# Which PSUM banks the convolution's norm uses, and where the first chunk's pieces land

## The chip, the cores and the metric

The kernel runs on one core of one Trainium2 chip. The metric is the device time of one execution in microseconds (us), as the median of several runs. A profiled execution gives the trace of that core.

## The reference

The reference is one layer of a conformer-like block on 256 tokens of width 1024, all in float32:

```
x = x + 0.5 * swiglu(rms_norm(x), w_gate, w_up, w_down)            # FFN 1, inner width 2816
proj = rms_norm(x) @ w_in                                           # 1024 -> 7168
a, b, q, k, v, gate_a, gate_b = split(proj)
u = causal_depthwise_conv(a * sigmoid(b))                           # 31 taps, 1024 channels
y_a = silu(layer_norm(u) * gain + bias) @ w_conv_proj
y_b = attention(rms_norm(q), rms_norm(k), v) @ w_attn_proj          # 16 heads of 64, causal
x = x + (sigmoid(gate_a) * y_a + sigmoid(gate_b) * y_b) @ w_out
x = x + 0.5 * swiglu(rms_norm(x), w_gate2, w_up2, w_down2)          # FFN 2
```

With 256 tokens and blocks of 256 the attention has one block, so only its causal own part is computed.

## The kernel before, in words

**Products.** Every product is made with operands split in two: `hi` is the value rounded to a short float32 form, `lo` is the rest. A product is the sum of three: activation hi x weight hi, activation hi x weight lo, activation lo x weight hi. The function `gemm` (L137) loads a piece of weights, two slices of 128 input rows by 512 columns, from memory into a "raw" buffer (SP issues the load, L151), rounds it to `hi` on ScalarE (ACT, L100), subtracts to make `lo` on VectorE (DVE) or GpSimd (POOL) (L102), and runs for each of two token halves and each slice three 128x512 matmuls on TensorE (PE, L165 to L167). The buffers "raw", "hi" and "lo" are rings of five. A chunk is 512 output columns: its products over all input rows end in two accumulators, one for each token half.

**PSUM.** The eight banks have three uses, each a ring: three banks "acc" for `gemm`, three "tr" for transposes and attention, two "cv" for the convolution and, at the very start, for the first chunk.

**The start.** The first chunk of FFN 1 has a function of its own, `gemm_first` (L106). Its eight pieces hold 512 columns of weights for one slice and, except the first, that slice of the transposed input (256 columns). Each goes through a "raw" buffer; ACT scales and rounds the input (L125), DVE makes its rest (L126), ACT rounds the weights and DVE makes their rest (L100, L102), PE runs six products into the two "cv" banks (L132 to L134). The second chunk goes through `gemm`; the loads of x and of the constants are queued on SP behind the second chunk's last piece (L597).

**The mixing block.** The projection `w_in` has 14 chunks. Between their products the kernel interleaves the attention of eight head pairs (score L465, flip L512, value L529, whose result ACT copies at L220), all in "tr" banks, and the convolution (L347, on DVE, one tap at a time for two channel slices into two "cv" banks, which ACT copies out at L350). A generator per channel group goes on a list, and `gemm` pumps a few steps of it after each piece. Behind the last convolution `conv_norm` (L352) stands on that list: for each token half two groups of four transposes into a "tr" bank (L359), a copy to SBUF by ACT (L364), statistics on DVE (L368, L370), the power -1/2 on POOL (L187) and the normalization on DVE (L375).

**The end of the mixing block.** Two chunks of the attention's projection (`w_attn`) follow; behind the last attention block ACT applies the sigmoid to gate b (L703), and DVE multiplies each accumulator by it (L714). Ahead of the second chunk the program places `conv_act` (L378): four times four transposes back into a "tr" bank (L385), SiLU on ACT (L392), rounding on ACT (L398) and the rest on DVE (L399). Its SiLUs are ordered behind the sigmoids of gate b, and the sigmoids of gate a behind what it returns, since each change between the two functions makes ACT load a table. Then come the convolution's projection (`w_conv`, two chunks, DVE L722 and L723) and `w_out`.

**What sets the order.** The program is written once in order; a planner then simulates the engines and fixes the order of each engine's queue. An instruction earlier in the program goes first among those that the planner takes to be ready, and a tile takes a buffer of its ring when its first writer is placed. On the chip each queue is executed in that fixed order.

Of the kernel before, what the change touches and what calls it, by code (L numbers as in the profile page):

```python
# [11 lines left out]
F32 = mybir.dt.float32  # L12
# [5 lines left out]
P = 128  # L18
S = 256
D = 1024  # L20
KD = D // P
# [7 lines left out]
CH = 512  # L29
# [6 lines left out]
KP = 2  # L36
RAW_BUFS, HI_BUFS, LO_BUFS = 5, 5, 5
# [13 lines left out]
class Build:  # L51
# [54 lines left out]
    def gemm_first(self, x0, w0, rest, hT):  # L106

        nc = self.nc
        acc = [self.cv(), self.cv()]
        hTh, hTl = hT  # L110
        ah, al = self.parts(*hT)
        for k in range(KD):
            raw = self.wp.tile([P, KP * CH], F32, tag="raw", name="raw", bufs=RAW_BUFS)
            hi = self.wp.tile([P, KP * CH], F32R, tag="hi", name="hi", bufs=HI_BUFS)
            lo = self.wp.tile([P, KP * CH], F32R, tag="lo", name="lo", bufs=LO_BUFS)
            if k == 0:
                nc.sync.dma_start(x0, self.io["x0"])
                nc.sync.dma_start(raw[:, :CH], w0)
                xk = x0[:, KD:]
            else:  # L120
                self.last_dma = nc.sync.dma_start(raw[:, : CH + S], rest[:, k - 1, :])
                xk = raw[:, CH : CH + S]
            g = x0[:, k : k + 1]
            sl = slice(k * S, (k + 1) * S)
            nc.scalar.activation(hTh[:, sl], xk, AF.Copy, scale=g)  # L125
            nc.vector.scalar_tensor_tensor(  # L126
                hTl[:, sl], xk, g, hTh[:, sl].bitcast(F32), ALU.mult, ALU.subtract
            )
            self.split(raw[:, :CH], hi[:, :CH], lo[:, :CH], False)
            for t in range(2):  # L130
                o, st, sp = acc[t], k == 0, k == KD - 1
                nc.tensor.matmul(o, ah(k, t), hi[:, :CH], start=st, stop=False)  # L132
                nc.tensor.matmul(o, ah(k, t), lo[:, :CH], start=False, stop=False)
                nc.tensor.matmul(o, al(k, t), hi[:, :CH], start=False, stop=sp)  # L134
        return acc

    def gemm(self, w, c, n, kt, ah, al, pump=0, pool=0.0, split_k=None, side=None):  # L137
# [214 lines left out]
    def conv_norm(self, yT, ynat):  # L352
        nc = self.nc
        for t in range(2):
            for c0 in range(0, KD, 4):
                ps = self.tr()
                for q in range(4):
                    c = c0 + q
                    nc.tensor.transpose(  # L359
                        ps[:, q * P : (q + 1) * P],  # L360
                        yT[c // 2][:, (c % 2) * S + t * P : (c % 2) * S + (t + 1) * P],
                        self.ident,
                    )
                nc.scalar.copy(ynat[:, t * D + c0 * P : t * D + (c0 + 4) * P], ps)  # L364
                yield 1
            st = self.tmp.tile([P, 2, 6], F32, tag="bst", name="bst", bufs=2)
            for c in range(2):
                nc.vector.bn_stats(st[:, c, :], ynat[:, t * D + c * CH : t * D + (c + 1) * CH])  # L368
            mv = self.tmp.tile([P, 2], F32, tag="mv", name="mv", bufs=2)
            nc.vector.bn_aggr(mv, st)  # L370
            r = self.rsqrt_mean(mv[:, 1:2], 1, 1)
            yield 1
            for c in range(2):
                y = ynat[:, t * D + c * CH : t * D + (c + 1) * CH]
                nc.vector.tensor_scalar(y, y, mv[:, 0:1], r, ALU.subtract, ALU.mult)  # L375
            yield 1

    def conv_act(self, ynat, hi, lo, after):  # L378
        nc = self.nc
        cst = self.cst  # L380
        for c in range(0, KD, 2):
            ps = self.tr()
            for q in range(2):
                for t in range(2):
                    nc.tensor.transpose(  # L385
                        ps[:, q * S + t * P : q * S + (t + 1) * P],
                        ynat[:, t * D + (c + q) * P : t * D + (c + q + 1) * P], self.ident,
                    )
            z = self.tmp.tile([P, CH], F32, tag="junk", name="z", bufs=2)
            with self.tc.issue_after(after.ins):  # L390
                for q in range(2):
                    last = nc.scalar.activation(  # L392
                        z[:, q * S : (q + 1) * S], ps[:, q * S : (q + 1) * S], AF.Silu,
                        bias=cst[:, C_LB + c + q : C_LB + c + q + 1],
                        scale=cst[:, C_LG + c + q : C_LG + c + q + 1],
                    )
            h = hi[:, c * S : (c + 2) * S]
            nc.scalar.copy(h, z)  # L398
            nc.vector.tensor_tensor(lo[:, c * S : (c + 2) * S], z, h.bitcast(F32), ALU.subtract)  # L399
        return last  # L400


    def head_norm(self, acc, rstd, c, dst, gain, rq=None):
# [437 lines left out]
```

## Time and profile before

| what | us |
|---|---|
| median of 3 runs | 647.08 |
| lowest and highest | 646.92, 647.13 |
| profiled execution | 647.48 |
| its span in the trace | 645.6 |

Times in the trace are counted from the start of the span. The profiled execution has its own time, 647.48; the span is what the instructions take, and the rest lies around it. A line of the timeline gives start, duration, engine, line of the kernel and operation, the tile written and those read, how many instructions were merged, and in brackets the idle time of the engine before it and what ended it. A matmul's duration includes the filling and emptying of the array, so starts, not durations, tell the pace of PE.

### The profile page before, as it was taken

What the parts mean: (1) busy time and instruction counts of PE and PEld (TensorE: products, weight loads), DVE (VectorE), ACT (ScalarE), POOL (GpSimd) and SP (SyncE); (2) the same over time, 40 slices, a digit from 0 to 9 for tenths busy, and PEclk for the clock granted to TensorE, in tenths of its full rate; (3) what the DMA queues carried; (4) which work ended last, traced back from release to release, by engine and by line L of the source; (5) the groups of instructions that cost most, each with busy time, mean ns of one, the idle gap of its engine ahead of it and who ended that gap; (6) DMA issues with size and microseconds to landing.
All of it is one profiled execution on the core that took longest, in us unless ns stands there. A gap on an engine that the chain in (4) does not pass through costs nothing.

```text
span 645.6 us, 8133 instructions
## 1 busy us (share of the span) xinstructions
PE 634.2 (98%) x2952; PEld 516.8 (80%) x2952; DVE 369.9 (57%) x625; ACT 362.5 (56%) x547; POOL 164.9 (26%) x83
## 2 busy tenths in 40 slices
PE   9999999999999999999999997899999999999997
PEld 7788888888888888777777785788888888888886
DVE  5655464554542699879313936485664546465541
ACT  6755354443545676987876667744655435444330
POOL 0100000000006999689866761000100000000000
PEclk9999999999999999999999999799999999999999
DMA  8966556567564555545654552264755656556630
GB/s 271 354 232 192 199 173 195 160 198 219 174 201 135 178 170 180 171 130 169 196 158 135 164 168 96 96 199 153 224 163 186 196 177 198 189 168 200 197 124 32
DMA packets 32855, 114.97 MB, mean 178 GB/s; under 512 B 3632, under 2 KB 4912, under 8 KB 32816
## 3 DMA queue, kind: packets, MB, share of 16 engines
q1 hardware_dynamic: 32816, 114.46, 55.9%
q8 instruction: 23, 0.38, 0.2%
q14 instruction: 16, 0.13, 0.1%
HBM read 113.40 MB, written 1.05 MB: 177 GB/s over the span
## 4 chain that ended last, share of the span: by engine, by line
PE 64%; DVE 2%; ACT 1%; issue 0%; DVEq 0%
PE acc L165 20%; PE acc L166 20%; PE acc L167 19%; PE tr L465 1%; PE tr L211 1%; PE tr L529 1%; PE tr L512 1%; DVE lo L102 1%; PE tr L438 1%; DVE bst L368 0%; ACT gate_b L703 0%; ACT z L392 0%; PE tr L655 0%; DVE gate_b L714 0%; ACT L703 0%
## 5 line engine op out<-in xcount | busy, mean ns | idle before, releaser
L100 ACT CAST hi<-raw 128x1024 fp32r<-128x1024 f32 (+1 forms) x216 | 223.1, 1035 | 220.3 <-PE acc L167 184.4
L102 DVE TENSOR_TENSOR lo<-raw,hi 128x1024 fp32r<-128x1024 f32 (+1 forms) x156 | 186.2, 1197 | 167.2 <-ACT hi L100 162.7
L102 POOL TENSOR_TENSOR lo<-raw,hi 128x1024 fp32r<-128x1024 f32 x60 | 143.7, 2420 | 200.3 <-ACT hi L100 200.2
L347 DVE SCALAR_TENSOR_TENSOR cv<-uT,cst,cv 128x255 f32<-128x255 f32 (+28 forms) x240 | 95.2, 465 | 8.4 <-ACT cv L343 8.2
L166 PE MATMUL acc<-lo,h1h 128*128 128x512 f32 x224 | 88.3, 394 | 0.0
L165 PE MATMUL acc<-hi,h1h 128*128 128x512 f32 x224 | 88.0, 398 | 0.2 <-DVE un L646 0.2
L167 PE MATMUL acc<-hi,h1l 128*128 128x512 f32 x224 | 87.3, 393 | 0.0
L165 PE MATMUL acc<-hi,h2h 128*128 128x512 f32 x176 | 69.1, 393 | 0.0
L165 PE MATMUL acc<-hi,aTh 128*128 128x512 f32 x176 | 68.8, 391 | 0.0
L167 PE MATMUL acc<-hi,aTl 128*128 128x512 f32 x176 | 68.5, 389 | 0.0
L166 PE MATMUL acc<-lo,aTh 128*128 128x512 f32 x176 | 68.5, 389 | 0.0
L166 PE MATMUL acc<-lo,h2h 128*128 128x512 f32 x176 | 68.5, 390 | 0.0
L167 PE MATMUL acc<-hi,h2l 128*128 128x512 f32 x176 | 67.2, 390 | 0.0
L166 PE MATMUL acc<-lo,hTh 128*128 128x512 f32 x160 | 62.4, 390 | 0.5 <-DVE lo L102 0.5
L165 PE MATMUL acc<-hi,hTh 128*128 128x512 f32 x160 | 62.2, 392 | 0.0
L167 PE MATMUL acc<-hi,hTl 128*128 128x512 f32 x160 | 62.2, 389 | 0.0
L165 PEld LDWEIGHTS acc<-hi,h1h 128*128 128x128 f32 x224 | 42.1, 188 | 10.3 <-issue 0.7
L167 PEld LDWEIGHTS acc<-hi,h1l 128*128 128x128 f32 x224 | 42.1, 188 | 9.3 <-issue 0.7
L166 PEld LDWEIGHTS acc<-lo,h1h 128*128 128x128 f32 x224 | 42.1, 188 | 8.9 <-issue 0.8
L167 PEld LDWEIGHTS acc<-hi,aTl 128*128 128x128 f32 x176 | 33.0, 188 | 6.9
L165 PEld LDWEIGHTS acc<-hi,aTh 128*128 128x128 f32 x176 | 33.0, 188 | 6.8
L165 PEld LDWEIGHTS acc<-hi,h2h 128*128 128x128 f32 x176 | 33.0, 188 | 6.8
(138 smaller groups left out, 778.8 us busy)
## 6 DMA issues: line engine op xcount, KB each, us to landing
raw<-w_in SPq DMA_DIRECT2D x56, 512.0 KB, 4.2
raw<-w2gu SPq DMA_DIRECT2D x44, 512.0 KB, 4.4
raw<-w1gu SPq DMA_DIRECT2D x40, 512.0 KB, 4.8
raw<-w1d SPq DMA_DIRECT2D x22, 512.0 KB, 4.3
raw<-w2d SPq DMA_DIRECT2D x22, 512.0 KB, 4.4
raw<-w_attn SPq DMA_DIRECT2D x8, 512.0 KB, 4.2
raw<-w_conv SPq DMA_DIRECT2D x8, 512.0 KB, 4.0
raw<-w_out SPq DMA_DIRECT2D x8, 512.0 KB, 4.4
```

Source lines behind the costliest of these rows:

```text
L100: nc.scalar.copy(hi, raw)
L102: ins = eng.tensor_tensor(lo, raw, hi.bitcast(F32), ALU.subtract)
L165: nc.tensor.matmul(o, ah(k, t), wh, start=st, stop=False)
L166: nc.tensor.matmul(o, ah(k, t), wl, start=False, stop=False)
L167: nc.tensor.matmul(o, al(k, t), wh, start=False, stop=sp)
L211: nc.tensor.transpose(ps[:, q * S + t * P : q * S + (t + 1) * P], src(t, j + q), self.ident)
L347: nc.vector.scalar_tensor_tensor(o, u, w, o, ALU.mult, ALU.add)
L438: nc.tensor.transpose(ps[:, q * S + t * P : q * S + (t + 1) * P], xs[t][:, (j + q) * P : (j + q + 1) * P], self.ident,)
L465: ins = nc.tensor.matmul(ps[q][:, t * P : t * P + (t + 1) * P], qT[r, b * S + t * P : b * S + (t + 1) * P], kT[r, b * S : b * S + (t + 1) ...
L512: nc.tensor.transpose(ps[:, i * P : (i + 1) * P], pr[:, o : o + P], self.ident)
L529: ins = nc.tensor.matmul(ps[q * HD : (q + 1) * HD, kt * P : S], v[:, kt * D + h * HD : kt * D + (h + 1) * HD], pT[:, o : o + n], start=kt ...
```

## The change

Three edits. The first chunk's pieces land in four tiles of 128x2048 of the pool that also holds the activations (two pieces in each), in place of "raw" buffers. Its products come in another order: for both token halves those with `hi` weights, then those with `lo` weights. The transposes of `conv_norm` and `conv_act` go to "cv" banks in place of "tr" banks, and `conv_act` returns its last rounding in place of its last SiLU, so that the sigmoids of gate a are ordered behind that.

```diff
@@ gemm_first
-            raw = self.wp.tile([P, KP * CH], F32, tag="raw", name="raw", bufs=RAW_BUFS)
+            if k % 2 == 0:
+                pair = self.big("first")
+            raw = pair[:, (k % 2) * 1024 : (k % 2) * 1024 + CH + S]
...
             for t in range(2):
-                o, st, sp = acc[t], k == 0, k == KD - 1
-                nc.tensor.matmul(o, ah(k, t), hi[:, :CH], start=st, stop=False)
-                nc.tensor.matmul(o, ah(k, t), lo[:, :CH], start=False, stop=False)
-                nc.tensor.matmul(o, al(k, t), hi[:, :CH], start=False, stop=sp)
+                nc.tensor.matmul(acc[t], ah(k, t), hi[:, :CH], start=k == 0, stop=False)
+                nc.tensor.matmul(acc[t], al(k, t), hi[:, :CH], start=False, stop=False)
+            for t in range(2):
+                nc.tensor.matmul(acc[t], ah(k, t), lo[:, :CH], start=False, stop=k == KD - 1)
@@ conv_norm
-                ps = self.tr()
+                ps = self.cv()
@@ conv_act
-            ps = self.tr()
+            ps = self.cv()
...
-                    last = nc.scalar.activation(
+                    nc.scalar.activation(
                         z[:, q * S : (q + 1) * S], ps[:, q * S : (q + 1) * S], AF.Silu,
...
             h = hi[:, c * S : (c + 2) * S]
-            nc.scalar.copy(h, z)
+            rounded = nc.scalar.copy(h, z)
             nc.vector.tensor_tensor(lo[:, c * S : (c + 2) * S], z, h.bitcast(F32), ALU.subtract)
-        return last
+        return rounded
```

## Rows read from the trace of the kernel before

**Rows 1.** The page, busy us, share of the span and instructions of PE.
```profile
PE 634.2 (98%) x2952; PEld 516.8 (80%) x2952; DVE 369.9 (57%) x625; ACT 362.5 (56%) x547; POOL 164.9 (26%) x83
```
**Rows 2.** Timeline of PE, first and second chunk.
```profile
10.96 0.61 PE L132 MATMUL cv<-hi,hTh 128*128 128x512 f32 x2
...
16.40 0.67 PE L165 MATMUL acc<-hi,hTh 128*128 128x512 f32 x2
17.60 0.50 PE L166 MATMUL acc<-lo,hTh 128*128 128x512 f32 x1 [0.53 <-DVE lo L102]
```
**Rows 3.** Timeline of ACT, first and second chunk.
```profile
8.55 0.60 ACT L100 CAST hi<-raw 128x512 fp32r<-128x512 f32 x1
...
15.24 1.05 ACT L100 CAST hi<-raw 128x1024 fp32r<-128x1024 f32 x1 [2.24 <-PE cv L134]
```
**Rows 4.** Timeline of SP's queue, second chunk's loads.
```profile
9.91 3.32 SPq L151 DMA_DIRECT2D raw<-w1gu  x4
```
**Rows 5.** Windows: busy PE, PEld, DVE, ACT, POOL; granted clock, DMA share, GB/s.
```profile
5.00:10.00 5.00, 5.00 (x21) 3.18 (x19) 3.90 (x8) 3.90 (x8) 0.00 (x0) 1.00 0.96 352
10.00:15.00 5.00, 5.00 (x23) 4.17 (x23) 3.88 (x8) 3.00 (x7) 0.00 (x0) 1.00 0.92 266
```
**Rows 6.** Windows of the end of the mixing block, columns as above.
```profile
381.60:388.70 7.10, 7.10 (x44) 5.09 (x43) 0.42 (x1) 1.31 (x4) 3.84 (x2) 1.00 0.62 205
...
392.00:394.00 2.00, 1.34 (x7) 0.61 (x6) 0.91 (x2) 2.00 (x6) 0.00 (x0) 1.00 0.00 0
...
404.00:406.00 2.00, 0.82 (x4) 0.82 (x5) 1.59 (x3) 0.00 (x0) 0.00 (x0) 0.50 0.95 336
...
410.00:412.00 2.00, 2.00 (x9) 1.58 (x8) 0.00 (x0) 1.98 (x4) 0.00 (x0) 0.86 0.02 4
```
**Rows 7.** Timeline of PE, end of the mixing block.
```profile
388.59 1.09 PE L359 MATMUL tr<-ident,uT 128*128 128x128 f32 x8
...
391.73 0.95 PE L167 MATMUL acc<-hi,ol 128*128 128x512 f32 x3
393.11 0.66 PE L359 MATMUL tr<-ident,uT 128*128 128x128 f32 x4 [0.43 <-ACT ynat L364]
394.43 0.50 PE L165 MATMUL acc<-hi,oh 128*128 128x512 f32 x1 [0.66 <-DVE gate_b L714]
...
401.50 0.76 PE L385 MATMUL tr<-ident,ynat 128*128 128x128 f32 x3 [1.33 <-ACT ms L185]
405.18 3.13 PE L385 MATMUL tr<-ident,ynat 128*128 128x128 f32 x13 [2.93 <-DVE ynat L375]
408.62 0.80 PE L165 MATMUL acc<-hi,u2h 128*128 128x512 f32 x1 [0.30 <-ACT u2h L398]
...
410.49 0.44 PE L165 MATMUL acc<-hi,u2h 128*128 128x512 f32 x1
```
**Rows 8.** Timeline of ACT, end of the mixing block.
```profile
377.55 0.37 ACT L350 COPY uT<-cv 128x256 f32<-128x256 f32 x1
...
388.71 0.37 ACT L220 CAST oh<-tr 128x256 fp32r<-128x256 f32 x1 [4.41 <-PE tr L529]
...
390.39 2.19 ACT L703 ACTIVATE gate_b<-gate_b 128x512 f32<-128x512 f32 x4
392.49 1.54 ACT L364 COPY ynat<-tr 128x512 f32<-128x512 f32 x3
...
406.12 1.93 ACT L392 ACTIVATE z<-tr,cst 128x256 f32<-128x256 f32 x4 [3.43 <-PE tr L385]
407.94 1.15 ACT L398 CAST u2h<-z 128x512 fp32r<-128x512 f32 x2
```
**Rows 9.** Timelines of DVE and POOL, the norm.
```profile
393.09 0.69 DVE L368 BATCH_NORM_STATS2 bst<-ynat 128x6 f32<-128x512 f32 x1 [3.55 <-ACT ynat L364]
...
404.59 1.00 DVE L375 TENSOR_SCALAR ynat<-ynat,mv,rs 128x512 f32<-128x512 f32 x2
...
401.48 1.88 POOL L187 TENSOR_TENSOR rs<-ms,neghalf 128x1 f32<-128x1 f32 x1 [1.38 <-ACT ms L185]
```

## The prediction

> **What bounds the kernel now.** I read the page first, for the share of each engine: TensorE (PE) is busy for 98% of the span [rows 1], so time can only come from stretches in which it waits or runs slowly. Then the busy time by windows, to find those stretches, the timeline of PE around them, and the timelines of the engines that PE waits for.
>
> The pace of PE is read from the first chunk: the step k = 4 starts at 10.96 and the next chunk at 16.40 [rows 2]; 24 products lie between, so one 128x512 product costs 5.44 / 24 = 0.227 us when nothing waits.
>
> The first stretch is the start. The third product of the second chunk starts at 17.60, where 16.40 + 2 x 0.227 = 16.85 was possible: 0.75 us, ended by the subtraction that makes the low weights [rows 2]. ScalarE (ACT) began to round that piece only at 15.24 after 2.24 idle us [rows 3]. The row names PE as the releaser, but the load was issued at 9.91 [rows 4] and the stretch 10 to 15 us moved 266 GB/s against 352 in the five before [rows 5]: I read it as a late landing. SP issued it late because the first chunk's eight pieces go through the five "raw" buffers.
>
> The second stretch is the end of the mixing block, around the convolution's norm. The windows show PE busy for 0.82 of 2 us in 404 to 406 and a granted clock of 0.50 there, that is 1.2 of 2.4 GHz; it is back during 410 to 412 [rows 6]. In PE's timeline the first half of the attention projection ends with three products from 391.73, PE then waits 0.43 us in front of the last four transposes at 393.11 and 0.66 us more for an accumulator, works from 394.43, falls idle near 400.2, does three transposes at 401.50, waits 2.93 us, in which the clock falls, does 13 at half clock, and reaches the convolution's projection at 408.62 and full pace at 410.49 [rows 7].
>
> Why so late? The convolution is done when ACT copies its last accumulator at 377.55. The norm's transposes run at 388.59, and their copies at 392.49, behind the last attention copy (388.71), a table load and four sigmoids (to 392.5) [rows 7, 8]. Between 381.6 and 388.7 ACT was busy for 1.31 of 7.10 us and VectorE (DVE) for 0.42 [rows 6]: the norm could have been done there, and what stood in the way was a bank, as all three "tr" banks serve the last attention blocks, which come earlier in the program. The statistics start at 393.09, the last normalization ends at 405.6, after other work of DVE [rows 9], and the SiLU that waits for it at 406.12 [rows 8].
>
> **The change part by part.**
>
> *Pieces in four large tiles.* No transfer, byte or instruction is added; the eight loads keep their order on SP's queue. Gone are SP's waits for a "raw" buffer, so the second chunk's four pieces, then x and the constants, are issued some five us earlier. The large tiles come from a pool of twelve of which few are in use then; I cost them at nothing. If the queue keeps 352 instead of 266 GB/s from 10 to 15 us, it is 0.43 MB, that is 1.2 us, further on by 15 us [rows 5]: the first piece lands near 13.9, its rounding takes 1.05 [rows 3] and its subtraction 1.3 (17.60 less the end of the rounding at 16.29) [rows 2, 3], together 16.3, before PE asks for it at about 16.5. Gain 0.75; the bounds are 0 (it lands as late as now) and 0.86 (with the pipeline restart of 0.11 behind a wait). I take 0.75, near the upper one.
>
> *Low products last.* Within a step the products with rounded weights come first, and DVE has four of them, 0.9 us, to make the low parts. The count of products is the same. The first steps stay bound by their loads: the rounded weights of step 3 end at 8.55 + 0.60 = 9.15 [rows 3]; from there six products take 1.36 and a restart 0.11, so step 4 starts at 10.62, not at 10.96 [rows 2]: 0.34. Bounds 0 and 0.4. Start in all: 1.1 us.
>
> *Norm in the "cv" banks.* The convolution is done with its two banks at 377.9 [rows 8]. From then the four groups of four transposes (0.43 us each, by eight in 0.85 from 388.59 [rows 7]) and the four copies (0.5 each [rows 8]) can run, two banks in turn, while attention keeps its three. This adds no work; 2 us of copies move ahead of the sigmoids into ACT's idle 5.8 us. They go past the last attention blocks' copies on ACT; if these slipped by up to 2 us, PE still has other products to do until the value product. The last copy ends near 385; then statistics 0.7, the power on GpSimd (POOL) 1.9, and two normalizations 1.0 [rows 9] give 388.6, say 390 as POOL is then also making low weights. That is before the sigmoids are over at 392.5, so the SiLU starts after the sigmoids and a table load of 1.3 (as between 389.1 and 390.4 now) at 393.8, its first pair takes 1.0 and its rounding 0.6 [rows 8]: the first operand is there at 395.4.
>
> *PE's path then.* From 392.5 (391.73 plus three products and a restart): the last group of transposes 0.43, 24 products of the second half 5.44, the 16 transposes of the activation at 0.107 each 1.7, together 7.6: the projection starts at 400.1. At full pace the start of today, read back from 410.49 by four products, is 409.6. The most to be had is 9.5 us; the least is nothing. I leave 1.1 in: 0.7 for the accumulator, which must wait for the gate's product on DVE, and 0.4 for restarts. ACT needs 1.6 + 1.05 = 2.6 us for a pair of operand and weights, PE 2.7 for its products, so ACT keeps up, 4.7 us ahead. Gain 8.4.
>
> *Sigmoid after the last rounding.* The last two roundings stood behind a table load and four sigmoids, 3.4 us; now these stand behind the roundings. Their result is wanted when 48 products are done, 10.9 us after the projection's start, so the move costs nothing.
>
> Sum: 1.1 + 8.4 = 9.5. The profiled execution took 647.48 (span 645.6, 1.9 around it), 0.4 above the median of 647.08; the gain is the same against either: 637.98 for that execution, **637.6** for the median.
>
> **The rivals.** What can be told from no change is 0.2%, 1.3 us: faster is below 645.8, slower above 648.4.
>
> *PE's fixed order (0.17).* The order is made ahead. If the activation's transposes are put in front of the second half's products, the third group waits for the first SiLU pair (393.8 + 1.0 = 394.8) and the fourth for the next pair and its bank, about 1.1 later, with 24 products queued behind. That costs 2 us; with the normalization late too, behind low weights on DVE and POOL as it is now, up to 6.5. For it: just this happens today at 401.50 and 405.18. Against it: the copies come 8 us earlier. 639.5 to 644, likeliest 641.5.
>
> *The clock falls all the same (0.08).* Only two banks serve 32 transposes, so PE stops often and briefly. The price by rows: 13 transposes took 3.13 instead of 1.39, and four products lost 0.96 [rows 7], so 2.7 us and 640.3. Against it: the two waits around 393 left the clock at 1.00 in 392 to 394 [rows 6]; it fell only after the long stretch without work. The Trainium skill ("TensorE: Matmul & The Clock Gate", A second HAM failure mode: psum-queue depth-cycling) tells of a kernel that idled a little between groups as it went round PSUM's banks, and whose clock went up and down for it. By that rule the sum would be 6.8, by the rows 9.5; the trace does not bear it out.
>
> *Only the start moves (0.08).* The order could leave the norm where it is, if what holds it is the lateness that the planner reckons with, and not the bank. Then 1.1: 646.0.
>
> *Slower: two banks for three (0.07).* With the order left as it is, the third group of transposes at 391.4 has no bank until the first copy ends at 393.0, and the products behind it wait; the fourth comes behind the next copy, and the rounding between the copies on ACT (1.05) pushes the statistics. The activation loses too: its third and fourth group wait for SiLU pairs, 0.6 us more before the projection, at half clock. In all some 2.7 us against 1.1 gained: 648.7. It decides if the norm's copies still stand behind the sigmoids. Against it: the idle banks after 377.9.
>
> **How the numbers follow.** The forecast has 0.60; with the first two rivals 0.85 lies below 645.8, 0.08 within 0.2%, 0.07 above. The lower end takes the upper bounds, 9.5 + 0.86 + 0.4 = 10.8, so 636.3, and 0.3 for scatter: 636.0. The upper end takes in the first two rivals: 644.0; what is left out is 0.15 and the forecast's own misses.
>
> **What would show it.** In the profile after: a start of the second chunk's first product near 16.05 and no wait at its third; the norm's copies on ACT before 388; statistics before 392; no granted clock of 0.50 between 395 and 415; the convolution's projection at full pace by 400 to 401 less the 1.1 of the start. Copies still behind the sigmoids would make the middle wrong; copies early, but long waits of PE in front of the activation's transposes, would be the fixed order; a rounding of the second chunk that still starts near 15 would make the start wrong.

## The result and the profile after

| | before | after |
|---|---|---|
| median of the runs (range, number) | 647.11 us (646.92 to 647.91, 4) | 641.03 us (639.92 to 642.60, 4) |
| profiled execution, span | 647.48, 645.6 us | 641.79, 640.0 us |
| predicted | | 637.6 us (636.0 to 644.0) |

The changed kernel is faster: the ratio is 0.9905 (95% interval 0.988 to 0.9931), 6.1 us less by the medians. The prediction had 9.5 less. The direction and the range held, but the sum behind them did not: of its two terms the small one turned round, from 1.1 us gained to 3.75 lost in the profiled executions, and the large one came out above its 8.4: 9.4 in these executions, 8.7 by the medians of its own experiment.

Most lines of the kernel before stand two lines further down in the kernel after (L165 is L167, L350 is L352); the three products of `gemm_first`, L132, L133 and L134, are now L133, L136 and L134. In the experiments the line numbers shift with each edit: go by the tiles and the loads.

**The page.** First the shares of the engines and the granted clock in 40 slices of the kernel after:

```profile
PE 631.7 (99%) x2952; PEld 516.8 (81%) x2952; DVE 370.1 (58%) x625; ACT 361.9 (57%) x547; POOL 162.7 (25%) x83
...
PEclk8999999999999999999999999999999999999999
```

PE has as many instructions as in [rows 1] and is busy for 2.5 us less, in a span that is 5.6 shorter. The one slice with a lower clock is the first: the dip that was in the mixing block is gone, and there is one at the start.

**The start.** The timeline of SP's queue, one row of the kernel before that was not shown yet:

```profile
1.65 7.06 SPq L121 DMA_DIRECT2D raw<-w1f  x7
```

and the same queue of the kernel after:

```profile
1.65 0.42 SPq L123 DMA_DIRECT2D first<-w1f  x1
2.11 0.91 SPq L153 DMA_DIRECT2D raw<-w1gu  x2
3.07 3.49 SPq L123 DMA_DIRECT2D first<-w1f  x6
7.79 1.59 SPq L153 DMA_DIRECT2D raw<-w1gu  x2
```

The reader is to look at the order. Before, the first chunk's seven later pieces went out in one row. Now two loads of the second chunk (`raw<-w1gu`, 512 KB each) stand at 2.11, between the first chunk's second and third piece. The third piece lands behind 1 MB that nobody wants yet. Who waits for that shows in ACT's timeline, first before, then after:

```profile
6.61 0.51 ACT L125 ACTIVATE hTh<-raw,x 128x256 fp32r<-128x256 f32 x1 [0.33 <-DMA raw<-w1f]
```

```profile
10.00 0.51 ACT L127 ACTIVATE hTh<-first,x 128x256 fp32r<-128x256 f32 x1 [3.87 <-DMA first<-w1f]
```

This is the first work on the third piece: at 10.00 instead of 6.61, 3.4 us later. By the windows below, 337 GB/s moved in this stretch, so by this estimate 1 MB is 3.1 us: the order alone would account for nearly all of it. PE's timeline of the kernel after:

```profile
7.26 0.63 PE L136 MATMUL cv<-lo,hTh 128*128 128x512 f32 x2
11.07 0.74 PE L133 MATMUL cv<-hi,hTh 128*128 128x512 f32 x2 [3.18 <-ACT hi L100]
...
13.10 1.05 PE L133 MATMUL cv<-hi,hTh 128*128 128x512 f32 x2
...
15.52 0.63 PE L133 MATMUL cv<-hi,hTh 128*128 128x512 f32 x2
...
21.01 0.62 PE L167 MATMUL acc<-hi,hTh 128*128 128x512 f32 x2
21.46 0.39 PE L168 MATMUL acc<-lo,hTh 128*128 128x512 f32 x1
```

and the windows of the kernel after (columns as in [rows 5]), of the start and, below the dots, of the end of the mixing block:

```profile
5.00:10.00 5.00, 2.89 (x12) 1.98 (x11) 1.48 (x3) 1.02 (x3) 0.00 (x0) 1.00 0.97 337
10.00:12.00 2.00, 0.93 (x4) 0.80 (x5) 1.44 (x3) 2.00 (x5) 0.00 (x0) 0.98 1.04 418
12.00:14.00 2.00, 2.00 (x7) 1.52 (x6) 2.00 (x5) 2.00 (x5) 0.00 (x0) 0.50 1.04 421
14.00:16.00 2.00, 2.00 (x8) 1.58 (x7) 2.00 (x5) 2.00 (x5) 0.00 (x0) 0.66 1.02 416
...
381.60:388.70 7.10, 7.10 (x43) 5.54 (x42) 2.02 (x4) 5.86 (x14) 6.53 (x3) 1.00 0.42 135
392.00:394.00 2.00, 2.00 (x14) 1.22 (x13) 0.44 (x2) 0.85 (x3) 0.55 (x1) 1.00 0.09 37
404.00:406.00 2.00, 2.00 (x11) 1.66 (x10) 2.00 (x4) 2.00 (x3) 0.00 (x0) 1.00 0.40 115
```

PE waits 3.18 us in front of the third piece, and behind the wait the granted clock falls to 0.50. The 12 products from 11.07 to 15.52 take 4.45 us, where 12 x 0.227 = 2.72 is the full pace: 1.73 lost to the clock. The second chunk starts at 21.01 instead of 16.40 [rows 2], 4.61 later (3.18 + 1.73, less 0.30 that the earlier steps won). But its third product follows at 21.46 without a wait, at 21.01 + 2 x 0.227, so the 0.86 of [rows 2] is indeed gained: 4.61 - 0.86 = **3.75 lost**. The last copy of the convolution confirms it: 381.30 below against 377.55 [rows 8], again 3.75.

**The middle.** All times of this stretch are to be read less 3.75. PE's timeline of the kernel after, which answers to [rows 7]:

```profile
384.57 0.60 PE L361 MATMUL cv<-ident,uT 128*128 128x128 f32 x4
...
394.74 0.38 PE L387 MATMUL cv<-ident,ynat 128*128 128x128 f32 x2
...
397.02 0.82 PE L387 MATMUL cv<-ident,ynat 128*128 128x128 f32 x6
...
403.13 1.04 PE L387 MATMUL cv<-ident,ynat 128*128 128x128 f32 x8
403.93 0.48 PE L167 MATMUL acc<-hi,u2h 128*128 128x512 f32 x1
```

ACT's, which answers to [rows 8]:

```profile
381.30 0.37 ACT L352 COPY uT<-cv 128x256 f32<-128x256 f32 x1
...
385.32 0.58 ACT L366 COPY ynat<-cv 128x512 f32<-128x512 f32 x1
...
390.03 1.08 ACT L366 COPY ynat<-cv 128x512 f32<-128x512 f32 x2 [0.98 <-PE cv L361]
393.33 0.37 ACT L222 CAST oh<-tr 128x256 fp32r<-128x256 f32 x1 [0.92 <-PE tr L531]
...
395.02 2.19 ACT L705 ACTIVATE gate_b<-gate_b 128x512 f32<-128x512 f32 x4
397.12 1.03 ACT L100 CAST hi<-raw 128x1024 fp32r<-128x1024 f32 x1
...
399.46 1.93 ACT L394 ACTIVATE z<-cv,cst 128x256 f32<-128x256 f32 x4
401.28 0.63 ACT L400 CAST u2h<-z 128x512 fp32r<-128x512 f32 x1
```

The norm's transposes now start 3.3 us behind the start of the convolution's last copy, and its copies run from 385.32 to 391.1, ahead of the sigmoids at 395.02; before, they came behind them. No row of PE between 380 and 410 shows a wait any more, the granted clock is 1.00 in each of the last three windows above, and the projection (`acc<-hi,u2h`) starts at 403.93 at full pace. Read back at full pace, the kernel before started it at 409.6, which with the lost start would be 413.35: **9.4 gained**. 9.4 - 3.75 = 5.65, and the profiled executions differ by 647.48 - 641.79 = 5.69.

### The profile page after: what moved, and what is told of

It is laid out like the page before. It is cut to its first block, busy times and chain, and to the rows that moved or that the text cites. A ratio compares the mean times of both kernels' runs of the same rounds, so it can differ in the third digit from the quotient of the medians.

```text
span 640.0 us, 8130 instructions
## 1 busy us (share of the span) xinstructions
PE 631.7 (99%) x2952; PEld 516.8 (81%) x2952; DVE 370.1 (58%) x625; ACT 361.9 (57%) x547; POOL 162.7 (25%) x83
## 4 chain that ended last, share of the span: by engine, by line
PE 66%; DVE 0%; DVEq 0%; issue 0%
PE acc L167 20%; PE acc L168 20%; PE acc L169 20%; PE tr L467 1%; PE tr L213 1%; PE tr L531 1%; PE tr L514 1%; PE tr L440 1%; PE tr L657 0%; PE cv L387 0%; PE cv L361 0%; DVE un L648 0%; DVE ot L756 0%; DVEq L832 0%
## 5 line engine op out<-in xcount | busy, mean ns | idle before, releaser
L100 ACT CAST hi<-raw 128x1024 fp32r<-128x1024 f32 x208 | 218.2, 1052 | 218.5 <-PE acc L169 193.6
L102 DVE TENSOR_TENSOR lo<-raw,hi 128x1024 fp32r<-128x1024 f32 x148 | 180.7, 1223 | 169.8 <-ACT hi L100 165.3
L167 PE MATMUL acc<-hi,h1h 128*128 128x512 f32 x224 | 88.0, 398 | 0.2 <-DVE un L648 0.2
L167 PE MATMUL acc<-hi,h2h 128*128 128x512 f32 x176 | 69.1, 393 | 0.0
L167 PE MATMUL acc<-hi,aTh 128*128 128x512 f32 x176 | 68.8, 391 | 0.0
L167 PE MATMUL acc<-hi,hTh 128*128 128x512 f32 x160 | 62.0, 392 | 0.0
L167 PEld LDWEIGHTS acc<-hi,h1h 128*128 128x128 f32 x224 | 42.1, 188 | 10.3 <-issue 0.7
L168 PEld LDWEIGHTS acc<-lo,aTh 128*128 128x128 f32 x176 | 33.1, 188 | 6.8
L167 PEld LDWEIGHTS acc<-hi,h2h 128*128 128x128 f32 x176 | 33.0, 188 | 6.8
```

The costliest lines, as they stand in the source:

```text
L100: nc.scalar.copy(hi, raw)
L102: ins = eng.tensor_tensor(lo, raw, hi.bitcast(F32), ALU.subtract)
L167: nc.tensor.matmul(o, ah(k, t), wh, start=st, stop=False)
L168: nc.tensor.matmul(o, ah(k, t), wl, start=False, stop=False)
```

## The experiments

Each kernel is compared with a median of the kernel before from the same chip: 647.55 for the whole norm edit, the whole edit of the start, the forced order of loads and `conv_norm` alone; 647.32 for the large tiles alone and for the least edit; 647.51 for the other four. A gain or loss is the difference of the medians.

**Which half gains, which loses?** The first kernel has the whole norm edit and the old start: `conv_norm` and `conv_act` in "cv" banks, and the rounding returned.

```diff
@@ conv_norm, conv_act
-                ps = self.tr()
+                ps = self.cv()
@@ conv_act
...
-        return last
+        return rounded
```

> The kernel before with the norm's and the activation's transposes in the cv banks and the sigmoid behind the last rounding; the first chunk as before. Theory A (the norm's edit is worth all of the 9.4 us by which the convolution's projection starts earlier, and the change lost 3.7 of it at the start): 637.7, with no granted clock of 0.5 after the first 5 us. Rival B (the two halves are not independent: the later start gave the other engines room that the norm used): 639 or more, with waits of PE between 385 and 400.

Measured: 638.89 (638.33 to 641.09), ratio 0.9875 (0.9851 to 0.9899): 8.7 gained. The time lies between the 637.7 of theory A and the 639 of rival B, and the profile decides for A: PE has no wait between 385 and 400, and the projection starts at 401.22. The start, which has no edit here, is 1.0 us later than in the profile of the kernel before (the convolution's last copy stands at 378.57, not at 377.55 [rows 8]), so the stage gained 409.6 + 1.0 - 401.2 = 9.4, as in the kernel after.

The second kernel has the edit of `gemm_first` alone, tiles and order of products both.

> The kernel before with the first chunk's edit alone (large tiles and low products last); norm in the tr banks. Theory A: the two loads of the second chunk that the planner put between the first chunk's second and third piece cost 3.7 us, of which some 1.7 are the half clock behind the wait: 650.8 (649 to 651). Rival B: the start is no slower by itself: 646 to 647.

Measured: 651.91 (651.28 to 652.66), ratio 1.007 (1.0052 to 1.0089): 4.4 lost, more than the 649 to 651 that was expected. Its profile has the wait, here longer, and the half clock of the kernel after (0.50 in the window 14 to 16 us). In PE's timeline:

```profile
12.38 0.72 PE L133 MATMUL cv<-hi,hTh 128*128 128x512 f32 x2 [3.91 <-ACT hi L100]
```

So the two edits pull in opposite directions. They don't add up exactly: -8.7 + 4.4 = -4.3, where the kernel after has -6.1. The start's loss is not the same in every execution. The four of the kernel after took 641.79, 639.92, 640.28 and 642.60, with a mean granted clock of 0.997, 0.999, 1.000 and 0.997: by these clocks the half clock behind the wait comes in some and not in others, while the four of the start alone all had 0.992. That is an inference for the executions without a profile, since a mean clock does not say where it was low (one of the four of the norm edit, 641.09, had 0.997 too). The next experiment has a profile of the case without the half clock.

**Is it the tiles or the order of the products?** Large tiles alone:

```diff
@@ gemm_first, in the loop over k
-            raw = self.wp.tile([P, KP * CH], F32, tag="raw", name="raw", bufs=RAW_BUFS)
+            if k % 2 == 0:
+                pair = self.big("first")
+            raw = pair[:, (k % 2) * 1024 : (k % 2) * 1024 + CH + S]
```

> The kernel before with the first chunk's pieces in the four large tiles and nothing else (old order of products, norm in tr). Theory A2 (the large tiles alone let the second chunk's loads past): the loss of the whole first-chunk edit, 651 to 652.5 against 647.5. Rival (the new order of products has a part in the loss, as a step is then held by other inputs): 648 to 650.

Measured: 651.38 (649.55 to 651.63, 8 runs), ratio 1.0054 (1.0038 to 1.0069): 4.1 lost. SP's queue shows the same order as in the kernel after:

```profile
2.11 0.91 SPq L153 DMA_DIRECT2D raw<-w1gu  x2
3.07 3.42 SPq L123 DMA_DIRECT2D first<-w1f  x6
```

Its profiled execution is the fastest of the eight, 649.55, and shows the price of the order without that of the clock:

```profile
10.98 0.73 PE L134 MATMUL cv<-hi,hTh 128*128 128x512 f32 x2 [2.52 <-ACT hi L100]
...
20.02 0.39 PE L168 MATMUL acc<-lo,hTh 128*128 128x512 f32 x1
```

PE waits 2.52 us here, the granted clock stays at 1.00 in every window from 10 to 20 us, and the second chunk's third product, the one at 17.60 before [rows 2], stands at 20.02: 2.4 lost. Five of the other seven executions took 651.4 to 651.6, about 2 more, with a mean granted clock of 0.992 against 0.995 in this one. So the loads out of order cost 2.4 us by themselves in this profile, and the half clock, where the mean clock tells of it, about 2 more.

The products of low weights last, alone:

```diff
@@ gemm_first, in the loop over k
             for t in range(2):
-                o, st, sp = acc[t], k == 0, k == KD - 1
-                nc.tensor.matmul(o, ah(k, t), hi[:, :CH], start=st, stop=False)
-                nc.tensor.matmul(o, ah(k, t), lo[:, :CH], start=False, stop=False)
-                nc.tensor.matmul(o, al(k, t), hi[:, :CH], start=False, stop=sp)
+                nc.tensor.matmul(acc[t], ah(k, t), hi[:, :CH], start=k == 0, stop=False)
+                nc.tensor.matmul(acc[t], al(k, t), hi[:, :CH], start=False, stop=False)
+            for t in range(2):
+                nc.tensor.matmul(acc[t], ah(k, t), lo[:, :CH], start=False, stop=k == KD - 1)
```

> The kernel before with the products of low weights last in each step of the first chunk, and nothing else; raw buffers, norm in tr. The prediction's term: step 4 starts 0.34 us sooner, but the second chunk's third product still waits for a landing that does not move, so that at most 0.3 us, and perhaps nothing, is left: 647.2 to 647.6 against 647.55. Rival: the order of products is worth its 0.34 and more because the second chunk's load is issued sooner with it: 646.5 to 647.

Measured: 647.58 (646.97 to 648.66, 10 runs), ratio 0.9999 (0.9987 to 1.0011): nothing. The wait for the second chunk's piece is still in PE's timeline, at its third product:

```profile
17.72 0.50 PE L166 MATMUL acc<-lo,hTh 128*128 128x512 f32 x1 [0.24 <-DVE lo L102]
```

The tiles make the loss; the order of products has no part in it that can be told.

**Is it the order of the loads?** The kernel after, with the second chunk's loads ordered behind the last load of the first chunk:

```diff
@@ gemm
-            self.last_dma = nc.sync.dma_start(
+            with self.tc.issue_after(self.last_dma.ins) if self.hold else nullcontext():
+              self.last_dma = nc.sync.dma_start(
@@ the call for the second chunk
+                        self.hold = True
                         u = self.gemm(wgu, c, n, KD, ah, al)
+                        self.hold = False
```

> The changed kernel with one edit: the second chunk's loads are ordered behind the first chunk's last piece on SP's queue. Theory A (the order of the loads is the whole loss): third piece rounded near 6.6 as before the change, second chunk's first product near 16.0 and no wait at its third, 636.6. Rival C (more loads in flight slow the early pieces, in whatever order they are issued): third piece after 8, second chunk not before 18, 639 or more.

Measured: 637.22 (636.98 to 637.52), ratio 0.9845 (0.9825 to 0.9864): 10.3 gained, the lowest median of the study. Its queue on SP:

```profile
1.65 3.51 SPq L124 DMA_DIRECT2D first<-w1f  x7
5.20 2.55 SPq L155 DMA_DIRECT2D raw<-w1gu  x4
```

PE's timeline, where the second chunk's third product follows its first two without a wait:

```profile
16.20 0.62 PE L169 MATMUL acc<-hi,hTh 128*128 128x512 f32 x2
16.66 0.39 PE L170 MATMUL acc<-lo,hTh 128*128 128x512 f32 x1
```

and the window that answers to the second of [rows 5]:

```profile
10.00:15.00 5.00, 5.00 (x24) 4.14 (x23) 3.90 (x8) 3.86 (x7) 0.00 (x0) 1.00 1.02 377
```

This is the start that was predicted. The second chunk's loads go out at 5.20 instead of 9.91 [rows 4], 4.7 us earlier; 377 GB/s are moved where it was 266; the second chunk starts at 16.20 (16.05 was predicted), and its third product stands at 16.66 instead of 17.60 [rows 2]: 0.94 gained, predicted 1.1. One pair of executions is weak evidence for the size, as the start scatters by up to 1 us: with the start of before, the third product stands at 17.60, 18.59, 17.82 and 17.90 (the kernel before, the norm edit, `conv_norm` alone, `conv_act` alone), and in the four profiles with the loads in order at 16.66, 17.49, 17.16 and 16.79. The means are 0.95 apart. Order and loss go together: with the order forced, nothing else changed, the loss is gone.

**Why did the loads change places?** My account: the first chunk's pieces wait for places in the pool of large tiles, which the planner gives out in the program's order of first writers; the second, third and fourth large tile stood behind the activations `hTh` and `hTl` there, whose first writers come after the first load. The "raw" buffers, now free, let the second chunk's loads pass. If so, it is enough to write the eight loads ahead of the loop that computes, with no order forced:

```diff
@@ gemm_first
+        raws = []
         for k in range(KD):
             if k % 2 == 0:
                 pair = self.big("first")
             raw = pair[:, (k % 2) * 1024 : (k % 2) * 1024 + CH + S]
...
+            raws.append(raw)
             if k == 0:
                 nc.sync.dma_start(x0, self.io["x0"])
                 nc.sync.dma_start(raw[:, :CH], w0)
...
             else:
                 self.last_dma = nc.sync.dma_start(raw[:, : CH + S], rest[:, k - 1, :])
...
+        for k in range(KD):
+            raw = raws[k]
...
```

The tiles `hi` and `lo` are taken in the second loop, where the rest of the old loop follows.

> The changed kernel with the first chunk's eight loads written ahead of its loop, with no order forced on SP. Theory A2 (the planner hands out the large pool's slots in the program's order of first writers: the second to fourth tile stood behind the activation tiles hTh and hTl, which ACT and DVE write only once x0 has landed, and the second chunk's loads, whose raw buffers were free, went past): the loads come in order and the time is that of the run with forced order, 637.2 (within 0.5). Rival (the forced order did something else too, such as holding back the loads of the second chunk): a time between 637.7 and 641.

Measured: 637.55 (636.90 to 637.97), ratio 0.9847 (0.9824 to 0.9869). SP's queue is in order again:

```profile
1.65 3.74 SPq L122 DMA_DIRECT2D first<-w1f  x7
5.43 3.50 SPq L156 DMA_DIRECT2D raw<-w1gu  x4
```

That supports the account; it does not prove it, since the planner's own book of places is in no profile.

**With the loads in order, does the order of products bring anything?** The kernel with forced order, with the old products (the diff of the low products above, reversed):

> The changed kernel with the second chunk's loads ordered behind the first chunk's, and the products of the first chunk in the old order (low weights in the middle). If the large tiles carry the start's gain: 637.2 plus at most 0.3. If the product order carries it: 638 or more, with PE waiting in front of the low products of steps 1 to 3 as before the change.

Measured: 637.58 (637.06 to 639.44), ratio 0.9856 (0.9825 to 0.9886), against 637.22 with the new order on another chip, and 637.55 for the kernel with the loads written ahead, which has the new order and ran on the same chip. The intervals of the ratios overlap almost wholly: the product order is worth nothing that can be told here either.

**Which part of the norm edit gains?** Only the transposes of `conv_norm` moved:

```diff
@@ conv_norm
-                ps = self.tr()
+                ps = self.cv()
```

> The kernel before with the transposes of the norm alone in the cv banks; the activation's stay in tr, and the sigmoid follows the last SiLU. Theory A (what was missing was a bank for the norm while attention held all three tr banks): the copies start before 388, and at least 8 of the 9.4 us are there: 637.7 to 639. Rival D (the activation's banks matter as much, since the last attention block and the transposes of the next stage share tr): 641 to 644.

Measured: 638.99 (638.69 to 639.45), ratio 0.9871 (0.9854 to 0.9888): 8.6 gained, as much as the whole norm edit. The first copy, in ACT's timeline, runs at 381.81, with only 0.24 to take off for the start (the convolution's last copy is at 377.79):

```profile
381.81 0.58 ACT L364 COPY ynat<-cv 128x512 f32<-128x512 f32 x1
```

Only the activation's transposes moved and the rounding returned, with `conv_norm` in "tr":

```diff
@@ conv_act
-            ps = self.tr()
+            ps = self.cv()
...
-        return last
+        return rounded
```

> The kernel before with the activation's transposes alone in the cv banks and the sigmoid behind the last rounding; the norm's transposes stay in tr. Theory A (the norm's copies stand behind the sigmoids for want of a bank, and the rest follows from that): the copies stay near 392.5, PE waits in front of the activation's transposes, and nothing is gained: 647 to 649, the upper end if two banks for three hold up the transposes. Rival D (the activation's banks carry a part of the gain): 641 to 645.

Measured: 647.84 (647.11 to 649.27, 10 runs), ratio 1.0009 (0.9997 to 1.0021): no gain, and no loss that can be told from none. PE's timeline has the long waits of the kernel before:

```profile
405.51 1.54 PE L385 MATMUL cv<-ident,ynat 128*128 128x128 f32 x6 [3.34 <-DVE ynat L375]
407.53 2.03 PE L385 MATMUL cv<-ident,ynat 128*128 128x128 f32 x8 [0.47 <-ACT z L392]
```

and one more, 0.47 us in front of the last eight transposes, whose releaser is a SiLU: with two banks they need one that it has read. That is the activation's part of the rival "two banks for three", by itself. It cost nothing in the end, since the clock was back sooner: the projection starts at 409.20 and is at full pace from its second product, 409.75, where the kernel before did its first four products at half clock, 408.62 to 410.49 [rows 7]. All of this stretch stands 0.33 later here (the norm's transposes at 388.92, not 388.59). Why the clock came back sooner was not tried.

**The least that gains all.** The eight loads written ahead with large tiles, and `conv_norm` in "cv"; the old order of products, the activation in "tr", the sigmoid where it was:

> The kernel before with two edits alone: the first chunk's pieces in the large tiles with their loads written ahead of the loop, and the norm's transposes in the cv banks; products in the old order, activation in tr, sigmoid behind the last SiLU. If these two carry everything: 637.2 to 637.9, within 0.1% of the runs with all the edits and the loads in order. If the activation's banks, the product order or the moved sigmoid add something once the rest is right: 638.2 or more.

Measured: 637.74 (637.47 to 639.68), ratio 0.9852 (0.9826 to 0.9877). Two of the edits, one of them mended, carry everything that can be told: the interval takes in the 0.9845 of the lowest median.

## Why the prediction was right in direction and wrong in size

- **"The eight loads keep their order on SP's queue": the step that failed.** I took the order from the program and looked only at the bytes. The same step says that SP's waits for "raw" buffers go, and costs the large tiles at nothing because few of the pool's twelve are in use. By the account above, which is supported and not proven, a free buffer is just what let the second chunk's loads pass, and a pool with room still gave its places in an order. The bounds of this term, 0 to 0.86, excluded a loss; none of the reasons given excluded a transfer that comes too early. By the runs the start was worth -3.75 in the profiled execution, the tiles alone -4.1 (-2.4 in the execution without the half clock), and the start with the order restored about +0.95, between 0.1 and 0.9 when each of its four profiles is set against the kernel before.
- **The mechanism behind "gain 0.75" held.** The second chunk's piece had indeed landed late, and loads issued earlier do take PE's wait away: there is no wait at the third product in the kernel after, nor in any of the six experiments with the large tiles. The row that named PE as the releaser [rows 3] is at odds with this, but with the low products last alone, the row of the same rounding names the load:

```profile
15.36 1.05 ACT L100 CAST hi<-raw 128x1024 fp32r<-128x1024 f32 x1 [1.54 <-DMA raw<-w1gu]
```

- **"Low products last", 0.34:** nothing could be measured, alone or with the loads in order. In the profile with this edit alone, the step k = 4 starts at 11.42 and not at 10.62, as the third piece came later (its first work is at 7.51, before at 6.61); so the term is neither seen nor ruled out, and its bounds, 0 to 0.4, hold by the medians at the lower one.
- **"Norm in the cv banks", 8.4: right in kind, a little too small.** By the medians the norm edit alone gained 8.7 and `conv_norm` alone 8.6. The profiled execution gained 9.4; the most that the prediction saw there was 9.5. The 1.1 held back for the accumulator and for restarts was not needed: where PE waited 0.66 for the accumulator [rows 7], six of the activation's transposes now run (397.02), so the order fills the gap. The copies came at 385.32 to 391.1, less 3.75 at 381.6 to 387.3, before the 388 that was named.
- **PE's path, 400.1:** 403.93 less 3.75 is 400.2. ACT's share of it was misjudged and covered: the first operand was ready at 401.28 + 0.63 - 3.75 = 398.2, not 395.4. The last attention copy was 0.9 later (393.33 - 3.75 = 389.6 against 388.71), a rounding of weights (397.12) went between sigmoids and SiLU, 1.0, and ACT did four SiLUs ahead of the first rounding and not two, 0.9. So its lead over PE was 2.0 us and not 4.7; had it been used up, PE would have waited.
- **"Sigmoid after the last rounding", 0:** not tried by itself. The least kernel without it is as fast, which agrees.
- **The rivals.** *PE's fixed order* did not come: all activation transposes ran without a wait. That agrees with the argument, that the copies come early. *The clock* did not fall in the middle, with 32 transposes through two banks at 1.00. The Trainium skill ("TensorE: Matmul & The Clock Gate", A second HAM failure mode: psum-queue depth-cycling) tells of a kernel whose clock went up and down through short idle times between groups of matmuls. PE has no such idle time here between 380 and 410, so this case does not test it. The clock fell instead where no rival looked, at the start, behind a wait of 3.18. *Only the start moves* is the reverse of what came. *Two banks for three* needed the copies to stay behind the sigmoids; with the activation alone moved they do stay there, and the kernel is then at 1.0009 (0.9997 to 1.0021) instead of slower by the 0.6 us that the prediction gave the activation's part.
- **The range** held the time because it reached to 644.0 for the first two rivals, neither of which came: that is luck. The lost 3.75 in place of 1.1 gained is 4.85, the 1.0 above 8.4 goes against it: 3.85 by the profiled execution, 637.98 + 3.85 = 641.8, which took 641.79. Where the start goes as predicted, the same sum is near: 637.22 measured, 637.6 predicted.

## What to carry to other kernels

When an edit frees buffers of a ring, ask which later loads can now start early, and on which queue they stand in front of loads that are wanted first; read the order of issue on that queue before trusting that more buffers only help. Work that waits for a bank of a busy ring, with another ring idle beside it, can be worth far more than its own time, since the stall that it ends took the clock with it: here 2 us of copies moved gained 8.6. And test the parts of a change apart: by its parts alone this one was a gain of 8.7 and a loss of 4.4, and mending the loss gave the lowest times, 637.2 to 637.7.

## What the runs showed of the hardware that was not expected

The power on GpSimd, 128 values, took 1.88 us in the kernel before [rows 9], and in the kernel after:

```profile
389.12 0.55 POOL L189 TENSOR_TENSOR rs<-ms,neghalf 128x1 f32<-128x1 f32 x1
...
392.49 0.55 POOL L189 TENSOR_TENSOR rs<-ms,neghalf 128x1 f32<-128x1 f32 x1 [2.82 <-ACT ms L187]
```

It is the same instruction on the same shape. In the trace VectorE was at work beside the slow one and not beside these two; whether that is the reason was not tried.

The half clock behind one wait at the start was in the profiled executions of the kernel after (wait of 3.18) and of the start alone (3.91), and not in that of the tiles alone (2.52, clock 1.00). By their mean granted clocks, executions of one kernel differ in it. In the profile of the kernel after it cost 1.73 us on top of the wait, and the kernel before, with waits of up to 2.93 in its middle, paid there too [rows 6, 7].

With the loads kept in order and issued ahead, 377 GB/s were moved in the window 10 to 15 us, where the kernel before, whose queue waited for buffers, moved 266 [rows 5].
